# Sliding windows: a band of 16 rows per partition, moved by 32-partition quadrants, in place of all rows of 8 channels moved over 128 partitions

## The chip, the cores and the metric

The kernel runs on 1 core of one Trainium2 chip. The metric is the device time in microseconds of one execution, lower is better. Most executions of one kernel agree within about one per cent; where they don't, the text says so. The granted clock was 1.0 in every run, and TensorE does nothing here.

## The reference, cut to what matters

```python
# x: (16, 64, 64, 64) float32 (batch, channel, row, column), window_size 8, stride 4
for i in range(15):
    for j in range(15):
        result[:, i, j] = x[:, :, 4*i:4*i + 8, 4*j:4*j + 8]
# result: (16, 15, 15, 64, 8, 8) float32
```

Nothing is computed. 16.78 MB are read, 58.98 MB are written. In the result the 64 channels of one window (batch, i, j) are 16 KB side by side: 256 bytes for each channel.

## The kernel before

A partition is one image and 8 channels, with all rows. A store takes one window place (i, j) for all images: 128 partitions x 2 KB.

```python
CHI = P // B            # 8
CLO = C // CHI          # 8 channels in a partition
gpool = ctx.enter_context(tc.tile_pool(name="gpool", bufs=28))
L = lpool.tile([P, CLO, H, W], f32)
...
nc.sync.dma_start(out=L[:, :, 0:HHALF, :], in_=x_v[:, :, :, 0:HHALF, :])
nc.sync.dma_start(out=L[:, :, HHALF:H, :], in_=x_v[:, :, :, HHALF:H, :])
trig = [nc.sync, nc.scalar]
for i in range(NH):
    for j in range(NW):
        g = gpool.tile([P, CLO, WS, WS], f32, name="g")
        src = L[:, :, i * ST : i * ST + WS, j * ST : j * ST + WS]
        nc.vector.tensor_copy(out=g[:, :, :, :], in_=src)
        trig[k % 2].dma_start(out=out[:, i, j, :, :, :], in_=g[:, :, :, :])
        k += 1
```

Of the kernel before, what the change touches and what calls it, by code (L numbers as in the profile page):

```python
# [1 line left out]

# [4 lines left out]


@with_exitstack  # L10
def kernel(
    ctx: ExitStack,
    tc: tile.TileContext,
    x: bass.AP,
    window_size: int,
    stride: int,
    out: bass.AP,
):
    nc = tc.nc
    P = nc.NUM_PARTITIONS  # L20

    B, C, H, W = x.shape
    Bo, NH, NW, Co, WSo, WSo2 = out.shape
    WS = int(window_size)
    ST = int(stride)
    assert Bo == B and Co == C and WSo == WS and WSo2 == WS

    f32 = mybir.dt.float32

    CHI = P // B  # L30
    CLO = C // CHI
    assert CHI * B == P and CLO * CHI == C

    lpool = ctx.enter_context(tc.tile_pool(name="lpool", bufs=1))
    gpool = ctx.enter_context(tc.tile_pool(name="gpool", bufs=28))

    L = lpool.tile([P, CLO, H, W], f32)

    HHALF = H // 2
    x_v = x.rearrange("b (ch cl) h w -> b ch cl h w", ch=CHI)  # L40
    nc.sync.dma_start(out=L[:, :, 0:HHALF, :], in_=x_v[:, :, :, 0:HHALF, :])
    nc.sync.dma_start(out=L[:, :, HHALF:H, :], in_=x_v[:, :, :, HHALF:H, :])

    trig = [nc.sync, nc.scalar]
    k = 0
    for i in range(NH):
        for j in range(NW):
            g = gpool.tile([P, CLO, WS, WS], f32, name="g")
            src = L[:, :, i * ST : i * ST + WS, j * ST : j * ST + WS]
            nc.vector.tensor_copy(out=g[:, :, :, :], in_=src)  # L50
            trig[k % 2].dma_start(out=out[:, i, j, :, :, :], in_=g[:, :, :, :])  # L51
            k += 1


# [1 line left out]
_INS = ['x', 'window_size', 'stride']  # L56
_OUTS = [((16, 15, 15, 64, 8, 8), 'float32')]
#: Inputs that are plain numbers.
_NUMBERS = {'window_size': 8, 'stride': 4}


# [26 lines left out]
```

## Time and profile before

| | before |
|---|---|
| time | 220.89 us (3 runs, 220.69 to 220.94) |
| span of the profile | 217.7 us |
| DVE busy | 88.7 us, 225 copies |
| DMA packets | 28800 stores of 2 KB, 2048 loads of 8 KB |
| rate while loading / while only storing | about 424 / about 355 GB/s |

How to read it: DVE is VectorE's name in the profile, and a packet is one piece that one DMA engine moves, here one run of bytes or the 4 bytes of a semaphore. The DMA row of the page is busy in nearly every slice and DVE is not, so the 16 DMA engines set the time; the GB/s row then tells how well they are used. The lines stand in the prediction. (Below, "the windows" of a run are stretches of its profile, not the sliding windows of the kernel.)

### The profile page before, as it was taken

Reading aid. Unit: us, or ns where it says so; the run is one execution under the profiler, and the core shown is the slowest. Engines: PE = TensorE matmul, PEld = TensorE weight load, DVE = VectorE, ACT = ScalarE, POOL = GpSimd, SP = SyncE. Lnnn points to the kernel's source line nnn. Section 1 sums busy time; section 2 is a strip of 40 time slices with the busy share of each in tenths; the row PEclk is TensorE's granted clock in tenths of the full one; section 3 lists DMA queues with packets and bytes.
Section 4 is the critical chain, followed back from the end, with each engine's and each line's share of the span. In section 5 each row is a group of like instructions: output and inputs, shape, how many; then the busy total and the mean of one; then the engine's idle time right before and its main releaser. Section 6 shows DMA issues by size and latency. Waiting matters only on the chain.

```text
span 217.7 us, 824 instructions
## 1 busy us (share of the span) xinstructions
DVE 88.7 (41%) x225; POOL 0.2 (0%) x4
## 2 busy tenths in 40 slices
DVE  0000691124532446454565555555554554550000
POOL 0000000000000000000000000000000000000000
DMA  6999999989995999999999999999999999999997
GB/s 200 431 425 422 422 423 429 416 311 318 339 345 166 287 321 356 349 353 361 353 358 362 364 354 354 358 355 365 345 341 334 363 363 347 349 343 337 329 338 252
DMA packets 34487, 75.83 MB, mean 348 GB/s; under 512 B 3632, under 2 KB 3632, under 8 KB 32432
## 3 DMA queue, kind: packets, MB, share of 16 engines
q1 hardware_dynamic: 18352, 46.41, 59.0%
q10 hardware_dynamic: 16128, 29.37, 39.2%
q14 instruction: 7, 0.06, 0.1%
HBM read 16.78 MB, written 58.98 MB: 348 GB/s over the span
## 4 chain that ended last, share of the span: by engine, by line
DMA 82%; DVE 7%; issue 1%; DVEq 0%; ACTq 0%
DMA out_dram<-g 72%; DMA L<-in_x_dram 10%; DVE g L50 7%; DVEq L50 0%; ACTq L51 0%
## 5 line engine op out<-in xcount | busy, mean ns | idle before, releaser
L50 DVE COPY g<-L 128x512 f32<-128x512 f32 x225 | 88.7, 424 | 108.0 <-DMA out_dram<-g 83.4
L69 POOL MEMSET const-bfloat16-1.0<- 128x1 bf16 x1 | 0.1, 102 | 0.0
L69 POOL MEMSET const-uint8-127<- 128x1 uint8 x1 | 0.1, 102 | 0.0
L69 POOL MEMSET const-float32-1.0<- 128x1 f32 x1 | 0.1, 99 | 0.0
L69 POOL MEMSET const-float32-0.0<- 128x1 f32 x1 | 0.1, 98 | 0.2 <-issue 0.2
## 6 DMA issues: line engine op xcount, KB each, us to landing
out_dram<-g SPq DMA_DIRECT2D x113, 256.0 KB, 5.5
out_dram<-g ACTq DMA_DIRECT2D x112, 256.0 KB, 5.2
L<-in_x_dram SPq DMA_DIRECT2D x2, 8192.0 KB, 33.9
```

Of the source, the lines that this page charges most:

```text
L50: nc.vector.tensor_copy(out=g[:, :, :, :], in_=src)
L69: nc = _bacc.Bacc("TRN2", target_bir_lowering=False, num_devices=1)
```

## The change

The intent is longer runs in the stores, 8 KB for 2 KB. A partition now holds half of the channels (32) of one image, but only a band of 16 rows; the four bands lie in the four quadrants of 32 partitions. Each quadrant has its own window row i, so each store is one quadrant: 32 partitions x 8 KB, again 256 KB. Quadrants 0 and 1 go over SyncE's queue, 2 and 3 over ScalarE's. Windows that cross into the next band are put together by copies from one quadrant to the next.

```diff
-    L = lpool.tile([P, CLO, H, W], f32)
+    L = lpool.tile([P, CL, RB, W], f32)          # 32 channels, 16 rows
+    x_v = x.rearrange("b (ch cl) (hq r) w -> hq (b ch) cl (r w)", ch=CH, hq=HQ)
+    o_v = out.rearrange("b i j (ch cl) r w -> i j b ch (cl r w)", ch=CH)
+    queues = [nc.sync, nc.sync, nc.scalar, nc.scalar]
+    for k in range(NCH):                          # 4 chunks of channels
+        for q in (0, 2, 1, 3):
+            queues[q].dma_start(
+                out=L[q * Q : (q + 1) * Q, k * cw : (k + 1) * cw, :, :],
+                in_=x_v[q, :, k * cw : (k + 1) * cw, :],
+            )
...
+    for j in range(NW):
+        for s in range(NSLOT):                    # 4 windows in a band
...
+                if not last:
+                    nc.vector.tensor_copy(out=g[:, cs, :, :], in_=L[:, cs, s * ST : s * ST + WS, cols])
+                else:
+                    nc.vector.tensor_copy(out=g[:, cs, 0:ST, :], in_=L[:, cs, s * ST : RB, cols])
+                    for q in range(HQ - 1):
+                        nc.vector.tensor_copy(
+                            out=g[q * Q : (q + 1) * Q, cs, ST:WS, :],
+                            in_=L[(q + 1) * Q : (q + 2) * Q, cs, 0:ST, cols],
+                        )
+                for q in (0, 2, 1, 3):
+                    i = NSLOT * q + s
+                    if i < NH:
+                        queues[q].dma_start(
+                            out=o_v[i, j, :, :, ...],
+                            in_=g[q * Q : (q + 1) * Q, cs, :, :],
+                        )
```

More of the change, by code (lines that the diff above doesn't have):

```diff
@@ L28 @@
     f32 = mybir.dt.float32
-    CHI = P // B
-    CLO = C // CHI
-    assert CHI * B == P and CLO * CHI == C
-    lpool = ctx.enter_context(tc.tile_pool(name="lpool", bufs=1))
-    gpool = ctx.enter_context(tc.tile_pool(name="gpool", bufs=28))
-    L = lpool.tile([P, CLO, H, W], f32)
-    HHALF = H // 2
-    x_v = x.rearrange("b (ch cl) h w -> b ch cl h w", ch=CHI)
-    nc.sync.dma_start(out=L[:, :, 0:HHALF, :], in_=x_v[:, :, :, 0:HHALF, :])
-    nc.sync.dma_start(out=L[:, :, HHALF:H, :], in_=x_v[:, :, :, HHALF:H, :])
@@ L44 @@
-    trig = [nc.sync, nc.scalar]
-    k = 0
-    for i in range(NH):
-        for j in range(NW):
-            g = gpool.tile([P, CLO, WS, WS], f32, name="g")
-            src = L[:, :, i * ST : i * ST + WS, j * ST : j * ST + WS]
-            nc.vector.tensor_copy(out=g[:, :, :, :], in_=src)
-            trig[k % 2].dma_start(out=out[:, i, j, :, :, :], in_=g[:, :, :, :])
-            k += 1
+    HQ = 4
+    CH = P // (B * HQ)
+    CL = C // CH
+    RB = H // HQ
+    Q = P // HQ
+    NSLOT = RB // ST
@@ new lines @@
+    assert Q == 32 and WS == 2 * ST
+    lpool = ctx.enter_context(tc.tile_pool(name="lpool", bufs=1))
+    gpool = ctx.enter_context(tc.tile_pool(name="gpool", bufs=9))
+    L = lpool.tile([P, CL, RB, W], f32)
+    x_v = x.rearrange("b (ch cl) (hq r) w -> hq (b ch) cl (r w)", ch=CH, hq=HQ)
+    o_v = out.rearrange("b i j (ch cl) r w -> i j b ch (cl r w)", ch=CH)
+    queues = [nc.sync, nc.sync, nc.scalar, nc.scalar]
+    NCH = 4
+    cw = CL // NCH
+    for k in range(NCH):
[4 more added lines that the diff above has]
+            )
@@ new lines @@
+    CFREE = CL * WS * WS
+    for j in range(NW):
+        cols = slice(j * ST, j * ST + WS)
+        for s in range(NSLOT):
+            g = gpool.tile([P, CL, WS, WS], f32, name="g")
+            chunks = NCH if j == 0 and s == 0 else 1
+            n = CL // chunks
+            last = s == NSLOT - 1
+            for k in range(chunks):
+                cs = slice(k * n, (k + 1) * n)
+                if not last:
[11 more added lines that the diff above has]
+                        queues[q].dma_start(
+                            out=o_v[i, j, :, :, k * CFREE // chunks : (k + 1) * CFREE // chunks],
+                            in_=g[q * Q : (q + 1) * Q, cs, :, :],
+                        )
```

## The prediction

> **What bounds the kernel now.** I read the page's header parts first (busy shares, the 40 slices, packets), then the chain that ended last, then the windows, then the packet records of the trace.
>
> ```profile
> DVE  0000691124532446454565555555554554550000
> DMA  6999999989995999999999999999999999999997
> GB/s 200 431 425 422 422 423 429 416 311 318 339 345 166 287 321 356 349 353 361 353 358 362 364 354 354 358 355 365 345 341 334 363 363 347 349 343 337 329 338 252
> DMA packets 34487, 75.83 MB, mean 348 GB/s; under 512 B 3632, under 2 KB 3632, under 8 KB 32432
> ...
> DMA 82%; DVE 7%; issue 1%; DVEq 0%; ACTq 0%
> DMA out_dram<-g 72%; DMA L<-in_x_dram 10%; DVE g L50 7%; DVEq L50 0%; ACTq L51 0%
> ...
> L50 DVE COPY g<-L 128x512 f32<-128x512 f32 x225 | 88.7, 424 | 108.0 <-DMA out_dram<-g 83.4
> ```
>
> The DMA row is at 9 in nearly every slice while DVE is half idle, and the copies wait 83.4 us for stores to free their buffers. The DMA engines set the time. The GB/s row shows two rates: about 424 while the 8 KB load packets run (slices 2 to 8), about 355 when only the 2 KB store packets run. So the stores run below what the same 16 engines do on loads although the engines are just as busy. The windows say it by stage, the third number from the end of each line being the share of busy DMA and the last the GB/s:
>
> ```profile
> core 0: us, DVE busy (x) POOL busy (x), PEclk, DMA share, GB/s
> 43.00:48.00 5.00, 1.24 (x3) 0.00 (x0) 1.00 0.83 328
> 48.00:56.00 8.00, 3.46 (x9) 0.00 (x0) 1.00 0.97 315
> 56.00:64.00 8.00, 3.51 (x9) 0.00 (x0) 1.00 1.01 340
> 64.00:75.00 11.00, 4.01 (x11) 0.00 (x0) 1.00 0.74 237
> 75.00:100.00 25.00, 12.01 (x32) 0.00 (x0) 1.00 1.02 342
> 100.00:150.00 50.00, 28.64 (x70) 0.00 (x0) 1.00 1.03 358
> ```
>
> There is a hole from 43 to 75 us. The timeline of the SyncE queue tells why: its first store is issued at 58.6 us. It had put both 8 MB loads on its own ring, and its first store waits for a store of the other queue whose semaphore it reuses; until then ScalarE's queue feeds the engines alone.
>
> The packet records, grouped by size, give what a packet costs one DMA engine. An 8 KB load packet takes 309 ns and the next starts 4 ns before its end: 305 ns each. A 2 KB store packet has a median of 84 ns, so 80 ns each. The line through the two is 5 ns + 75 ns per 2 KB. Beyond that line, in the pure store stage (80 to 200 us) the mean of a 2 KB packet is 94 ns: one packet in ten or more is stretched to about 150. One transfer gives each engine 8 packets (16 KB) and one 4-byte semaphore packet (9 ns). At 357 GB/s such a share takes 16384 x 16 / 357e9 = 734 ns: 640 for the packets, about 95 for stretch and semaphore. Following packets whose starts and ends fit together, the stretched one stands last before the semaphore more often than elsewhere (mean 121 against 92 ns, though the chains mix). While load packets alternate with store packets (24 to 43 us) no store packet is stretched at all.
>
> My ledger for before: first packet at 2.2 us; loads 2048 packets / 16 x 305 ns = 39.0; stores 225 x 0.734 = 165.2; last packet to end 1.3. Sum 207.7; the span is 217.7, so 10 us are lost, mostly in the hole.
>
> [...]
>
> **The change part by part.**
> 1. *Store runs of 8 KB instead of 2 KB.* 225 transfers of 256 KB stay 225. A share is 2 x 305 = 610 ns instead of 640: 30 ns. If stretch and semaphore stay at 85 ns per share (my choice between 20 and 120), it is 695 ns, 377 GB/s. 225 x 0.695 = 156.4, and the first slot's cutting in four adds 12 semaphores, 1.0 us. Stores 157.4 against 165.2: -8.
> 2. *Load runs of 4 KB instead of 8 KB.* 4096 packets / 16 x (5 + 150) ns = 39.7 against 39.0: +0.7, an estimate from the line above.
> 3. *The hole.* Both queues now load and store, the loads in 16 pieces, so neither queue is shut out as SyncE's was. But slot 1 copies need all channels, hence the last load. Then come a copy [...], an issue and the 1.5 us that the first load took from issue to first packet, partly under the first slot's last small stores. I put 2.5 us against 10: -7.5.
> 4. *Copies.* Per column three of 128x2048 [...], one of 128x1024 and three of 32x1024 across quadrants [...] against 15 transfers x 0.695 = 10.4. DVE stays hidden[...]. 9 buffers of four transfers are deeper than what is in flight (8 semaphores, so 8 transfers in both kernels).
> 5. *Issue.* 225 + 12 + 16 issues; an undisturbed one takes about 0.55 to 0.65 us in the trace. SyncE has 8 stores per column, 4.4 to 5.2 us of 10.4; ScalarE 7. Hidden, but SyncE's queue is the longer.
>
> Sum of the span: 2.2 + 39.7 + 2.5 + 157.4 + 1.3 = 203.1. Measured time is 3.2 over the span now (220.9 against 217.7): 206.
>
> **The rivals.**
> - *Ports.* Each engine serves 32-partition transfers; those of SyncE lie in quadrants 0 and 1, those of ScalarE in 2 and 3[...]. [...] If they often collide, packets of 8 KB show 500 to 600 ns instead of 309, and the mean falls to perhaps 300 GB/s: 75.8 MB / 0.30 = 253 us. [...]
> - *The memory side limits writes at about 357.* Stretched packets exist only in the pure store stage, and loads get 424 on the same engines. Then a share stays at 734 ns whatever the packet: stores 165, time about 214, 3% better, only from the hole.
> - *The stretch goes with packets.* Two packets instead of eight then leave some 25 ns of it: 635 ns per share, stores 144, time about 193.
>
> **Range and chances.** I give the sum (stretch per transfer) and its lighter version together about half, the write limit 0.25, the ports 0.2 to 0.25. Predicted 206 us, range 192 to 236. Faster by over 2% (under 216.5) 0.68; the write limit with a somewhat larger hole lands within 2%: 0.12; slower, which needs the ports, 0.20.
>
> **What would show it.** Step 1: GB/s in the pure store stage near 377, 8 KB packets at 309 ns except the one before a semaphore. Write limit: GB/s stays near 357 with both packets stretched. Ports: packets of 500 ns and more, also on the loads, whose stage would then last well over 42 us. Step 3: the slices around 42 us show one dip of 2 to 3 us. [...] I am wrong if 32-partition transfers don't overlap across quadrants, or if SyncE's longer queue runs alone for long.

What no run here shows is cut from the text above and marked: rules about engines and partitions, single copy times, and the arguments built on them. No term of the sum is cut: 2.2 + 39.7 + 2.5 + 157.4 + 1.3 = 203.1 us of span, 206 us of time. Three things in it are estimates:

- The 2.5 us of step 3. The trace shows the issue (0.55 to 0.65 us) and the 1.5 us to the first packet (issued at 0.73, moving at 2.18 us); the length of the copy that it also counts is cut, as the kernel before has no copy of 2048 elements.
- Division by 16 for 32-partition transfers. The changed kernel bears it out: 4048 small packets are its 253 transfers x 16 (before: 3632 = 227 x 16), and the mean busy share of the 16 engines was 1.03 from 10 to 40 us, while every transfer was a 32-partition load.
- For the rival *Ports*, 500 to 600 ns (up to about twice the 309 ns of the trace) and 300 GB/s.

No run shows a port. Packet counts behind two statements: from 45.8 to 58.6 us ScalarE's queue starts 2128 packets and SyncE's 11; from 24 to 43 us 841 load packets run with 566 store packets of 2 KB, and of those none takes over 102 ns, against 13% from 80 to 200 us.

## The result, and the profile after

The changed kernel takes 249.66 us (4 runs, 247.36 to 251.42) against 220.91 us (4 runs). The ratio of the fast runs is 1.126 (95% interval 1.119 to 1.132): 12.6% slower. Ratios here are the mean time of one kernel's fast runs over that of the other's fast runs of the same rounds, so not quite the ratio of the quoted medians. The profiled run took 251.42 us and counts as slow, being 1.6% over the fastest of four; the trace taken again later (249.46 us) shows the same stages.

First the page of the changed kernel: span, busy shares, rates and packets.

```profile
span 249.6 us, 659 instructions
...
DVE 96.0 (38%) x108; POOL 0.2 (0%) x4
...
DMA  7999999998999999999999999999999999999996
GB/s 205 290 291 291 295 296 290 290 291 240 260 331 320 319 327 322 328 331 331 335 328 337 305 344 327 336 330 339 330 330 322 316 323 324 324 324 327 248 211 139
DMA packets 15733, 75.82 MB, mean 304 GB/s; under 512 B 4048, under 2 KB 4048, under 8 KB 8656
```

The engines are as busy as before and still the bound, with half as many packets, but everything runs slower: the load at about 291 GB/s instead of 424, the stores at about 328 instead of 355, and the last three slices at 248 and less. The windows of the changed kernel by stage (busy share of DMA, then GB/s, at the end of a line):

```profile
core 0: us, DVE busy (x) POOL busy (x), PEclk, DMA share, GB/s
0.00:60.00 60.00, 1.28 (x3) 0.20 (x4) 1.00 0.99 284
60.00:75.00 15.00, 14.03 (x17) 0.00 (x0) 1.00 0.87 270
75.00:230.00 155.00, 80.66 (x89) 0.00 (x0) 1.00 0.95 328
230.00:249.60 19.60, 0.00 (x0) 0.00 (x0) 1.00 0.88 202
```

The copies wait for stores as before, so DVE is no part of it (groups of instructions of the changed kernel):

```profile
L66 DVE COPY g<-L 128x2048 f32<-128x2048 f32 (+1 forms) x48 | 55.0, 1159 | 110.1 <-DMA out_dram<-g 63.8
L70 DVE COPY g<-L 32x1024 f32<-32x1024 f32 x45 | 30.8, 684 | 1.1
L68 DVE COPY g<-L 128x1024 f32<-128x1024 f32 x15 | 10.4, 692 | 21.7 <-DMA out_dram<-g 21.7
```

The packet records say what happened to single packets. The 4 KB load packets have a median of 222 ns, where the prediction's line gives about 159. The 8 KB store packets from 100 to 200 us have a median of 309 ns, undisturbed, but a mean of 375; 15% take more than 500 ns, up to twice 309 and beyond. In the last 12 us, when ScalarE's queue is empty (its last packet starts at 232.6 us), 98% of the 8 KB packets take more than 500 ns (median 626) and the rate is 211 GB/s from 236 to 246 us.

The ledger against the prediction's sum of 203.1 us: the load's last packet ends at 59.9 us instead of 2.2 + 39.7 = 41.9, +18.0. From there to the last packet at 248.3 us are 188.4 us instead of 2.5 + 157.4, +28.5. Together +46.5, which is the whole difference to the span of 249.6. Of the second part about 20 us are the rate in the main stage (50.8 MB at 328 instead of 377 GB/s) and about 8 the end on one queue (3.96 MB in 18.3 us instead of 10.5).

### The profile page after: what moved, and what is told of

Its sections match the earlier page's. It is cut to its first block, busy times and chain, and to the rows that moved or that the text cites. A ratio compares the mean times of both kernels' runs of the same rounds, so it can differ in the third digit from the quotient of the medians.

```text
span 249.6 us, 659 instructions
## 1 busy us (share of the span) xinstructions
DVE 96.0 (38%) x108; POOL 0.2 (0%) x4
## 2 busy tenths in 40 slices
DMA packets 15733, 75.82 MB, mean 304 GB/s; under 512 B 4048, under 2 KB 4048, under 8 KB 8656
## 3 DMA queue, kind: packets, MB, share of 16 engines
q1 hardware_dynamic: 8224, 39.85, 50.8%
## 4 chain that ended last, share of the span: by engine, by line
DMA 75%; DVE 8%; SPq 4%; ACTq 2%; issue 1%; DVEq 1%
DMA out_dram<-g 52%; DMA L<-in_x_dram 23%; DVE g L66 4%; SPq L77 4%; DVE g L70 3%; ACTq L77 1%; DVE g L68 1%; ACTq L50 1%; DVEq L111 0%; DVEq L66 0%; DVEq L68 0%
## 5 line engine op out<-in xcount | busy, mean ns | idle before, releaser
L66 DVE COPY g<-L 128x2048 f32<-128x2048 f32 (+1 forms) x48 | 55.0, 1159 | 110.1 <-DMA out_dram<-g 63.8
L70 DVE COPY g<-L 32x1024 f32<-32x1024 f32 x45 | 30.8, 684 | 1.1
L68 DVE COPY g<-L 128x1024 f32<-128x1024 f32 x15 | 10.4, 692 | 21.7 <-DMA out_dram<-g 21.7
## 6 DMA issues: line engine op xcount, KB each, us to landing
L<-in_x_dram ACTq DMA_DIRECT2D x8, 1024.0 KB, 28.5
```

Of the source, the lines that this page charges most:

```text
L66: nc.vector.tensor_copy(out=g[:, cs, :, :], in_=L[:, cs, s * ST : s * ST + WS, cols])
L68: nc.vector.tensor_copy(out=g[:, cs, 0:ST, :], in_=L[:, cs, s * ST : RB, cols])
L70: nc.vector.tensor_copy(out=g[q * Q : (q + 1) * Q, cs, ST:WS, :], in_=L[(q + 1) * Q : (q + 2) * Q, cs, 0:ST, cols],)
```

## The experiments

Theory: **shared half**, the rival *Ports* or port theory. It is a hypothesis: 32-partition transfers that are under way together in the same half of the partitions (quadrants 0 and 1, or 2 and 3) hold each other up, to about twice the packet time and half the rate of 128 partitions; with the queues in different halves they do so less. What it is that they would share, no trace here shows; the runs show which partitions were moved together, and at what rate. Rivals: **run length** (4 KB load runs are slow), **number of transfers** and semaphores, **SyncE's longer queue** (120 windows against 105), and a **limit on writes to memory** near 357 GB/s.

### Both queues in the same half

```diff
-queues = [nc.sync, nc.sync, nc.scalar, nc.scalar]
+queues = [nc.sync, nc.scalar, nc.sync, nc.scalar]
-for q in (0, 2, 1, 3):        # load and stores
+for q in (0, 1, 2, 3):
```

> The changed kernel with the quadrants dealt out so that both queues work in the same half of the partitions at the same time (SyncE quadrants 0 then 2, ScalarE 1 then 3); transfers, sizes and counts are the same. Port theory [...]: the loads fall from 293 GB/s to about 200 to 210, 4 KB load packets from 221 ns to about 310, the load ends near 84 us; 8 KB store packets mostly near 620 ns while the queues keep in step, less where they drift apart; total 300 to 370 us. Rivals (4 KB load runs, the number of transfers, SyncE's longer queue): nothing of that changes, so 247 to 251 us and 293 GB/s in the load.

281.99 us (one run, correct; before 220.38). The windows of this run:

```profile
20.00:40.00 20.00, 0.43 (x1) 0.00 (x0) 1.00 1.03 210
...
100.00:150.00 50.00, 24.08 (x26) 0.00 (x0) 1.00 0.97 305
```

The same transfers, sizes and counts, dealt out otherwise, and the load falls from 293 to 210 GB/s: half of what the kernel before reaches (424). The 4 KB packets go from 222 to 324 ns (medians), and the load ends at 82.4 us. This is the number of the shared-half theory (200 to 210), and no rival on the list has one for it. The total was missed: 300 to 370 us were expected. In the stores the rate is 305, well above the 210 of the load; the expectation allowed for queues that drift apart, and whether they did is not shown.

### Short load runs over all partitions; long load runs by quadrant

The kernel before with its load cut into 4 KB runs, all 128 partitions:

```diff
-    nc.sync.dma_start(out=L[:, :, 0:HHALF, :], in_=x_v[:, :, :, 0:HHALF, :])
-    nc.sync.dma_start(out=L[:, :, HHALF:H, :], in_=x_v[:, :, :, HHALF:H, :])
+    for k in range(4):
+        nc.sync.dma_start(out=L[:, :, k * HQ4 : (k + 1) * HQ4, :],
+                          in_=x_v[:, :, :, k * HQ4 : (k + 1) * HQ4, :])
```

> The kernel before with its load cut into four row bands, so 4 KB runs, still over all 128 partitions. Port theory: 4 KB packets take about 159 ns (line through 2 KB and 8 KB) and the load runs at about 420 GB/s, total 215 to 222 us. Rival (short load runs are what slowed the load): about 220 ns and 293 GB/s as in the changed kernel, total about 235 us.

And with 8 KB runs, but by quadrant:

```diff
+    queues = [nc.sync, nc.sync, nc.scalar, nc.scalar]
+    for k in range(2):
+        for q in (0, 2, 1, 3):
+            ps, hs = slice(q * 32, (q + 1) * 32), slice(k * HHALF, (k + 1) * HHALF)
+            queues[q].dma_start(out=L[ps, :, hs, :], in_=x_v[ps, :, hs, :])
```

> The kernel before with its load kept at 8 KB runs but cut into 32-partition quadrants, 0 and 1 on SyncE's queue, 2 and 3 on ScalarE's, as the change does. Port theory: 8 KB load packets go from 309 to 430 to 450 ns and the load falls to about 290 to 300 GB/s, ending near 59 us. Rival (run length): 309 ns and 424 GB/s, load ends near 42 us.

222.3 us and 237.5 us (one run each, both correct). The rate row of the page, first of the short runs over 128 partitions, in slices of 5.5 us:

```profile
GB/s 208 418 411 410 408 313 410 416 344 350 420 358 300 182 308 336 344 351 348 342 322 354 359 355 352 352 346 341 336 344 353 359 356 354 344 329 350 326 344 205
```

Then of the long runs by quadrant, in slices of 5.9 us:

```profile
GB/s 142 245 261 252 266 257 254 264 253 260 263 286 406 399 374 355 346 341 334 333 344 335 346 364 356 353 341 359 363 362 340 342 364 361 358 357 354 362 367 249
```

Run length costs the load almost nothing: about 410 GB/s, 4 KB packets at a median of 159 ns, as the line of the prediction had it. Quadrants cost it 40%: 258 GB/s, and 8 KB packets at 507 ns instead of 309. The loss was even larger than expected (290 to 300 GB/s). In this run the stores, still over 128 partitions, go on at the rate of before.

### Queues of equal length

```diff
-    queues[q].dma_start(
+    queues[q if j % 2 == 0 else 3 - q].dma_start(
```

> The changed kernel with the two queues swapped in every second column, so that both have about the same number of stores (113 and 112 windows instead of 120 and 105). If SyncE's longer queue running alone at the end costs what the 230 to 250 us window shows (198 GB/s instead of 328, about 4 MB): 8 us less, about 241 us. If the tail only moves: 247 to 251 us. In either case it stays well over 221 us if ports are the main cause; if the imbalance were the main cause it would fall to about 206 us.

250.68 us median of 4 runs (all correct), but from 242.27 to 258.88. The windows of its profiled run (253.31 us):

```profile
20.00:40.00 20.00, 0.85 (x2) 0.00 (x0) 1.00 1.02 359
...
100.00:150.00 50.00, 24.48 (x27) 0.00 (x0) 1.00 0.97 289
```

The longer queue is not the main cause: without it the time stays 22 to 38 us over before. What it is worth by itself, 8 us or less, stays open, because the main stage ran worse in this trace (289 instead of 328 GB/s). The edit brings this about: at each change of column the queues swap halves, and while one of them is a column ahead, both work in the same half. Such a stretch between two others in the windows:

```profile
147.00:153.00 6.00, 2.41 (x2) 0.00 (x0) 1.00 0.99 355
153.00:158.00 5.00, 2.21 (x5) 0.00 (x0) 1.00 1.01 216
158.00:164.00 6.00, 2.49 (x3) 0.00 (x0) 1.00 0.93 310
```

To assign every 8 KB packet to its quadrant, count the bytes of each queue against the order of its stores. From 65 to 230 us both queues are then in the same half about a quarter of the time: there the packets have a median of 628 ns and 81% take more than 500; with the queues in different halves it is 309 ns and 17%. The rates, in steps of half a microsecond, average 225 and 322 GB/s. So within one run, with stores of one size, a packet takes twice as long in the median when the two queues share a half. This is the clearest evidence for the shared-half theory.

The load is unexpected: the very same load instructions as in the changed kernel, yet 359 instead of 293 GB/s.

> The changed kernel once more, for a second trace. Port theory [...]: the load, the same instructions, can run at another rate than the 293 GB/s of the first trace (the run with swapped queues had 359 in the same load), anywhere from 208 to 420, and the total moves with it by several us. If the load rate is set by the sizes alone: 290 to 296 again.

249.46 us (one run). Its load runs at 307 GB/s, its stores at 327 (windows):

```profile
20.00:40.00 20.00, 0.43 (x1) 0.00 (x0) 1.00 1.03 307
...
100.00:150.00 50.00, 25.48 (x28) 0.00 (x0) 1.00 0.95 327
```

So the same load has run at 293, 307 and 359 GB/s, each rate held from its first full slice to about its end, though sizes, counts and queues were equal. (The traces were not all taken on the same chip: 359 on chip 12, 307 on chip 8, the first not recorded.) What sets a run's rate, and what holds it, no run here shows.

### What 8 KB store runs are worth without quadrants

The next five runs keep the load and the copies of before, and write to the output seen as 128 equal stretches, one for each partition, 450 KB apart. Their outputs are wrong, which doesn't matter for the times. The 1 MB runs have 8 buffers of four windows instead of 28 of one. The cut below is shortened and put together from the five edits.

```diff
+    o_f = out.rearrange("b i j c r w -> (b i j c r w)").rearrange("(p f) -> p f", p=P)
+    run = CLO * WS * WS                      # 2 KB
-            trig[k % 2].dma_start(out=out[:, i, j, :, :, :], in_=g[:, :, :, :])
+        # base: one window, 256 KB
+        trig[m % 2].dma_start(out=o_f[:, m * run : (m + 1) * run], in_=g ...)
+        # 1 MB in 2 KB runs: windows m, m+56, m+112, m+168
+        dst = o_f[:, 0 : 4 * 56 * run].rearrange("p (n m f) -> p m n f", n=4, f=run)[:, m]
+        # 1 MB in 8 KB runs: four windows side by side
+        trig[m % 2].dma_start(out=o_f[:, m * 4 * run : (m * 4 + 4) * run], in_=g ...)
+        # the same, by quadrant
+        for q in (0, 2, 1, 3):
+            trig[q // 2].dma_start(out=o_f[32*q : 32*q+32, m * 4 * run : ...], in_=g[32*q : 32*q+32 ...])
+        # base, but partition (a, c) to stretch (c, a): dimensions 16 x 8
+        o_f = ....rearrange("(c a f) -> a c f", a=16, c=8)
```

> Result wrong on purpose: the kernel before, but every store goes to the output seen as 128 equal stretches, one for each partition, so 128 x 2 KB, 256 KB a store. Only the places in memory differ. It is the base for the next three. Each of the theories of the stretched 2 KB packet (per semaphore, memory side) expects about 350 to 360 GB/s between 100 and 150 us as before[...].

> Result wrong on purpose: as the base, but four windows in one store of 1 MB, still in 2 KB runs, so a quarter of the semaphores. Theory that the stretch comes with each semaphore: 390 to 400 GB/s in the pure store stage. Theory that the memory side limits writes, or that it goes with packets: 350 to 360 as in the base.

> Result wrong on purpose: four windows in one store of 1 MB, in 8 KB runs, over all 128 partitions. It shows what 8 KB store runs are worth [...]. Memory-side limit: 355 to 360 GB/s. Otherwise 410 to 425 with packets at 309 ns, and about 190 to 197 us in all.

> Result wrong on purpose: the same four windows, 8 KB runs and places in memory as the run before, but each 1 MB cut into four 32-partition stores dealt to the queues as the change does; the load stays over 128 partitions. Port theory: about 300 to 330 GB/s in the pure store stage with 8 KB packets up to 600 ns and more, 20% below the uncut 1 MB stores. If the cutting costs only its semaphores: within 5% of them.

> Result wrong on purpose: as the flat base with 2 KB runs (381 GB/s, hardly a packet over 102 ns), the same 128 places 450 KB apart, but which partition goes to which place is transposed, so that the memory side of a store has the dimensions 16 x 8 as in the kernel before instead of one dimension of 128. [...] the stretch comes back: about 350 to 360 GB/s, a tenth or more of the packets near 150 ns. If the places in memory made the difference (16 KB pieces side by side in the kernel before), it stays near 381.

The times are 203.56, 203.30, 187.71, 217.11 and 222.28 us (one run each). The windows show the pure store stage of each, in this order: base,

```profile
100.00:150.00 50.00, 27.84 (x71) 0.00 (x0) 1.00 1.04 381
```

1 MB in 2 KB runs,

```profile
100.00:150.00 50.00, 23.65 (x69) 0.00 (x0) 1.00 1.03 378
```

1 MB in 8 KB runs,

```profile
100.00:150.00 50.00, 24.96 (x72) 0.00 (x0) 1.00 1.01 419
```

the same by quadrant,

```profile
100.00:150.00 50.00, 24.15 (x68) 0.00 (x0) 1.00 0.98 346
```

and the base with dimensions 16 x 8:

```profile
100.00:150.00 50.00, 25.95 (x67) 0.00 (x0) 1.00 1.02 345
```

- 8 KB runs do what the change wanted: 419 against 378 GB/s with 1 MB stores, +11%. So 357 is not a limit on writes.
- The base was itself a surprise: 350 to 360 GB/s were expected of it if the stretched packet came with each semaphore or from a limit of the memory side; it ran at 381.
- Quadrants take it away again: 346 against 419, -17%, with the same runs to the same places, over a wide load. Their 8 KB packets have a median of 309 and a mean of 367 ns, 10% over 500, close to the changed kernel's 309, 375 and 15%. Cutting into quarters also means four times as many transfers; the second run, with a quarter of the base's transfers, shows that this number is worth hardly anything (378 against 381).
- The base has as many stores and semaphores as the kernel before (3632 small packets in both) and hardly a stretched packet (0.1% over 140 ns), so the stretch does not come with the semaphore. (The second run can't tell, because its base has no stretch to lose.)
- The 16 x 8 arrangement brings the stretch back: 10% of the 2 KB packets over 140 ns, against 0.1% in the base and 8.5% in the kernel before, and 345 GB/s. So the kernel before loses about 6% of its store rate (358 against 381) to the arrangement of its stores, not to the places that they fill. How the arrangement acts is not shown: the packet records name no engine, and the order in which the places are filled changed as well.

One rival stays untested: partitions that move together also fill places in memory together, so a clash on the memory side could follow the quadrants too. Against it speaks that loads of row bands (291 GB/s against 424), loads of whole images (258 against 424) and stores to two different layouts (328 and 346 against 419) all lost by quadrants.

### Closing the hole at the start of the kernel before

The prediction held that 10 us of the kernel before are lost, mostly from 43 to 75 us, where SyncE's queue was shut out. First only the second load moved to the other queue:

```diff
-    nc.sync.dma_start(out=L[:, :, HHALF:H, :], in_=x_v[:, :, :, HHALF:H, :])
+    nc.scalar.dma_start(out=L[:, :, HHALF:H, :], in_=x_v[:, :, :, HHALF:H, :])
```

> The kernel before with one change: its second 8 MB load is issued on ScalarE's queue instead of SyncE's, so that neither queue waits for the other's stores at the start. If the hole from 43 to 75 us (SyncE's first store at 58.6 us) cost the 10 us of the ledger: 210 to 214 us, and faster than both kernels. If the lost time lay elsewhere: 218 to 221 us.

217.49 us (4 runs, 215.07 to 218.86, two of them fast; before 220.84), ratio of the fast runs 0.978 (0.971 to 0.984), unclear at the 2% mark, and between the two expectations (210 to 214, or 218 to 221). SyncE's first store now goes out at 43.7 us instead of 58.6, but both halves of the load end together, so the copies start late and a dip remains:

```profile
40.00:50.00 10.00, 6.75 (x21) 0.00 (x0) 1.00 0.75 260
```

Then the load was cut so that each queue loads half of the channels of each row half:

```diff
+    for h in range(2):
+        for n, eng in enumerate((nc.sync, nc.scalar)):
+            hs, cs = slice(h * HHALF, (h + 1) * HHALF), slice(n * CHALF, (n + 1) * CHALF)
+            eng.dma_start(out=L[:, cs, hs, :], in_=x_v[:, :, cs, hs, :])
```

> The kernel before with its load cut by rows and by channels into four 4 MB pieces in 8 KB runs over all 128 partitions, one of each row half on each queue. Copies can start at about 22 us and neither queue is shut out. Moving the second load alone gave a ratio of 0.9775 and left a dip of about 4 us between 40 and 50 us (260 GB/s). If that dip goes: 212 to 215 us, ratio 0.96 to 0.975, and 340 GB/s or more between 40 and 50 us. If the copies' early start does not help: 216 to 218 us.

211.88 us (4 runs, 211.60 to 213.52; before 221.11), correct, ratio 0.962 (0.953 to 0.971): faster than both kernels. Windows:

```profile
40.00:50.00 10.00, 3.78 (x10) 0.00 (x0) 1.00 1.04 403
50.00:60.00 10.00, 5.26 (x15) 0.00 (x0) 1.00 1.04 373
60.00:75.00 15.00, 7.72 (x21) 0.00 (x0) 1.00 1.03 354
```

The hole (328, 315, 340, 237 GB/s before) is gone; after it the stores run at about 350 as before. Of the ledger's 10 us, 9 were had in this run (7.9 by the spans of the two profiles).

## Why the prediction was wrong, point by point

- **The chosen case.** The prediction centred on 206 us and called faster with 0.68. The rival *Ports*, at 0.20 to 0.25, described what came: packets of 500 to 600 ns and more, loads slowed too, 253 us against 249.66 measured. That its number came so close is partly luck: its 300 GB/s was a "perhaps", and the mean of 304 is made of 291 in the load, 328 in the main stage and 202 at the end. The step that failed is that the sum took the packet cost of 128-partition transfers (305 ns for 8 KB) for both the load and the store terms, without sharing; in the changed kernel the 8 KB packets of the main stage took 375 ns on average. The argument against the rival, that dealing the halves to different queues avoids the clash, was not shown; the first experiment shows that the dealing avoids part of it only (293 against 210 GB/s in the load, where 410 to 424 were to be had over 128 partitions).
- **Step 1, stores.** Per share 695 ns were assumed; at 328 GB/s it is 16384 x 16 / 328e9 = 799 ns. Without quadrants, in the run with 1 MB stores to the other layout, it is 626 ns (419 GB/s), so the gain from 8 KB runs was rather understated, near the 635 of the rival *The stretch goes with packets*; quadrants added 173.
- **Step 2, loads.** 155 ns per 4 KB packet was right over 128 partitions (159 ns long, with the 4 ns overlap of the prediction). In quadrants it was 222 ns. +18 us.
- **Step 3, the hole.** Right for the changed kernel: 13% of the 15 us from 60 to 75 us are idle, 2 us, against 2.5. That the hole of before is worth 8 to 9 us is shown by the last experiment.
- **Step 4, copies.** Right that they stay hidden behind the stores: DVE was busy 96.0 of 249.6 us, and its copies waited 85.5 us for stores. (Single copies took 1226 ns for 128x2048, 692 for 128x1024 and 684 for 32x1024.)
- **Step 5, issue.** SyncE's longer queue was named and not sized. Alone, in quadrants 0 and 1, it ran at 211 GB/s, close to half of 419 and to the 210 of the first experiment's load; about 8 us of the span by the ledger.
- **The stretched packets of before.** Kept as a cost per transfer, 85 ns with the semaphore, from chains said to mix. Wrong: with as many semaphores another arrangement of the stores removed it. It was a sign in the old trace that the same engines, equally busy, lose time by how a transfer is arranged (381 against 345 GB/s at DMA shares of 1.04 and 1.02).
- **From span to time.** The 3.2 us added at the end compares the span of one execution with the time of others. In every run the time is 1.7 to 1.8 us over its own span, so the sum of 203.1 stood for about 205 us. Against 249.66 this does not matter.

## What to carry to other kernels

Packet length and which partitions a transfer covers are two levers, and the second can outweigh the first: 8 KB runs were worth +11% (419 against 378 GB/s), cutting them into 32-partition quadrants -17% (346 against 419). When DMA engines are all busy and the rate is low, group the packet records by size and look for packets of about twice the common duration (here 626 against 309 ns); then change only which partitions move together, before changing the layout. And before any new layout, look for slices in which one queue stands still: here that gave 4% for a few lines.
